# Down projections of a two-layer decoder trunk: the high weights' two products joined into one of 512 columns

## Chip, cores and metric

The kernel runs on one core of a Trainium2 chip. The metric is the time of one execution on the device in microseconds, the median of several runs. The kernel before takes 1029.28 us (three runs, 1028.52 to 1032.02).

## The reference

Two layers over 256 tokens of width 1024, all in float32. Each layer has a mixer (a gated delta-rule branch with 8 heads, a sliding-window attention branch with 16 heads, and an output projection) and a gated MLP of width 2816 with a causal convolution. Both are conditioned: a vector c gives six modulation vectors for each layer. The part that matters here is the end of each layer:

```python
h = rms_norm(x, norm_ffn[l]) * (1.0 + sc2) + sh2
up_act, up_lin = jnp.split(h @ w_up[l], 2, axis=-1)
up_act = causal_dwconv(up_act, ffn_conv[l]) + ffn_conv_b[l]
x = x + gt2 * ((jax.nn.silu(up_act) * up_lin) @ w_down[l])
```

The change touches the product with `w_down`, the multiplication by `gt2` and the addition to x.

## The kernel before

**Layout.** x lies in SBUF as 8 tiles of 128 features by 256 tokens. A projection gives one output tile (128 features by 256 tokens) at a time: the weights are the stationary side, 128 x 128 for each k tile, and the activations the moving side, 256 columns.

**Three products for one.** To keep the accuracy of float32 with the faster type fp32r, every operand is split into a high part (rounded to fp32r) and a low part (the rest). A projection adds up high x high, high weights x low activations, and low weights x high activations; `mm3` (lines 281 to 284) issues these three for each k tile, in this order, into one PSUM tile:

```python
PE.matmul(o, wh, ah, start=first, stop=False)
PE.matmul(o, wh, al, start=False, stop=False)
PE.matmul(o, wl, ah, start=False, stop=last)
```

**Weights.** They come in chunks of 128 x 1024 float32 (8 k tiles) through a pool `raw` of 6 buffers, loaded by SyncE's queue (line 200). ScalarE casts a chunk to its high part `wH` (line 210), and VectorE subtracts to get the low part `wL` (line 212); each of these pools has 4 buffers. `weights()` hands out the next chunk and starts what is three chunks ahead. Two offsets (`SHIFT`) inside the wH and wL tiles alternate by a table `KICK`; chunks 0 and 12 of each layer's down projection have the second.

**The MLP.** For 22 tiles of the inner width the kernel computes both up projections, convolution and gate, and stores the result in `gp[i]`, a tile of 128 x 2 x 256: the high part at index 0, the low part at index 1, so that the two lie side by side (lines 1162 to 1204). They stand in the profile as `g_a` (i below 8) and `g_b`.

**The down projection** (lines 1210 to 1229) runs over 8 output tiles f. For each f three chunks of 8, 8 and 6 k tiles go through `mm3` into a PSUM tile of 256 columns, alternately from the pool `acc` and from `dnps` (3 buffers each, one PSUM bank of 512 float32 columns per buffer). Then one VectorE instruction, the eviction in line 1221, computes x = p * gt2 + x:

```python
V.scalar_tensor_tensor(x[:, f], p_, mod[l][:, 40 + f:41 + f], x[:, f], op0=ALU.mult, op1=ALU.add)
```

What follows differs by layer. In layer 0, ScalarE squares the new x tile (line 416), VectorE adds the squares up for the next norm (line 417), ScalarE makes the fp32r part `xH` (line 430) and VectorE its low part `xL` (line 431), and layer 1 begins with products of `xH` and `xL` whose last k tile needs the tile f = 7. In layer 1, the x tile is stored to `out` (line 1229).

**Modulation of the next layer.** In layer 0's down projection, `ada_step` fetches rows of `w_ada` into the same `raw` pool and lets VectorE multiply and sum them (line 328): 15 times in f = 1 to 5 and once in f = 6.

**What sets the order.** A scheduler fixes each engine's order when the program is built, by priorities (`tc.high_priority`) and its own estimates; the engines then work through their queues in order. Evictions, squares and `xH`/`xL` have a high priority, loads and splits of weights that of work done ahead.

Of the kernel before, what the change touches and what calls it, by code (L numbers as in the profile page):

```python
# [8 lines left out]
ALU = mybir.AluOpType  # L9
# [4 lines left out]
T = 256  # L14
# [5 lines left out]
FT = FF // P  # L20
# [79 lines left out]
def trunk(tc, xT, cvec, pos, wada, wsa, wbig, wdn, par, cst, out):  # L100
    nc = tc.nc
    V, A, G, PE = nc.vector, nc.scalar, nc.gpsimd, nc.tensor
# [20 lines left out]
    def acc(w=T, name="acc"):  # L123
        return accp.tile([P, w], F32, name=name, tag="acc")

    def ps(shape, name="ps"):
        return dnp.tile([P] + list(shape), F32, name=name, tag="dn")
# [23 lines left out]
    x = cp.tile([P, KT, T], F32, name="x")  # L151
# [64 lines left out]
    def weights():  # L216
        i = nextc["i"]
        nextc["i"] += 1
        while state["n"] < min(len(plan), i + 1 + LOOK):
            with tc.high_priority(offset=AHEAD):  # L220
                load_chunk(state["n"])
                split_chunk(state["n"])
            state["n"] += 1
        return got.pop(i)
# [56 lines left out]
    def mm3(o, wh, wl, ah, al, first, last):  # L281
# [4 lines that stand above are left out]
    def proj(ah, al, w=T, alt=False):  # L286

        wh, wl = weights()
        wh = wh.rearrange("p (k n) -> p k n", n=P)
        wl = wl.rearrange("p (k n) -> p k n", n=P)  # L290
        p_ = ps([w], name="acc2") if alt else acc(w)
        for kt in range(KT):
            mm3(p_, wh[:, kt], wl[:, kt], ah(kt), al(kt), kt == 0, kt == KT - 1)
            tick(BLOCK)
        return p_


    mod = [cp.tile([P, 48], F32, name=f"mod{l}") for l in range(NL)]
# [43 lines left out]
    def need(l, g, lo, hi):  # L342
        assert all((l, g, i) in done for i in range(lo, hi)), (l, g, lo, hi)
# [19 lines left out]
    def ada_step(n=1):  # L363

        for _ in range(n):
            while adaq and len(adaf) < 2:
                l, g, f = adaq.pop(0)
                adaf.append((l, g, f, ada_fetch(l, g * 8 + f)))
            if adaf:
                l, g, f, raw = adaf.pop(0)  # L370
                dot = ada_dot(l, g * 8 + f, raw)
                if behind:
                    after(dot, behind["op"])
                if f % 4 == 3:
                    ada_cols(l, g, f - 3, f + 1)
# [33 lines left out]
    def ssq_add(kt):  # L409
        if kt == 0:  # L410
            s = wk.tile([P, T], F32, name="ssq", tag="ssq", bufs=1)
            A.activation(s, x[:, 0], AF.Square)
            ssq["t"] = s
        else:
            q = t1("sqx")
            A.activation(q, x[:, kt], AF.Square)
            V.tensor_tensor(ssq["t"], ssq["t"], q, ALU.add)
# [106 lines left out]
    for l in range(NL):  # L524
# [6 lines left out]
        if l:  # L531
            ga[0] = quad("ga0")
            for f in range(4):
                with tc.high_priority(offset=HPN):
                    nrm.tile(f)
                t, c = rawx.proj(nrm.r, 0.5)
# [34 lines left out]
        else:  # L571
            for i in range(12):
# [4 lines left out]
                wh, wl = (t.rearrange("p (k n) -> p k n", k=2) for t in weights())  # L577
                for k4 in range(2):
                    kt = i // 3 * 2 + k4
# [57 lines left out]
        for q4 in range(4):  # L637
# [6 lines left out]
            for j in range(4):  # L644
# [3 lines left out]
                                   op0=ALU.mult, op1=ALU.add)  # L648
            exps.append(A.activation(dmat[:, q4 * 4:q4 * 4 + 4], dmat[:, q4 * 4:q4 * 4 + 4], AF.Exp))

        def at(t):
            return lambda kt: t[:, kt]
# [473 lines left out]
        for f in range(8):  # L1126
            y_ = yb[f // 4][:, f % 4]
            p_ = proj(at(sH), at(sL))
# [33 lines left out]
        gp = []  # L1162
# [7 lines left out]
        gH = lambda i: gp[i][:, 0]  # L1170
        gL = lambda i: gp[i][:, 1]
# [7 lines left out]
        for i in range(FT):  # L1179
# [8 lines left out]
            with tc.high_priority(offset=hpe):  # L1188
                g = t1("g")
                A.activation(g, pa_, AF.Identity, scale=fw[:, i, 2:3], bias=PR(l, "fbias", i, i + 1))  # L1190
                for sft in (1, 2):
                    V.scalar_tensor_tensor(g[:, sft:], pa_[:, :T - sft], fw[:, i, 2 - sft:3 - sft], g[:, sft:],  # L1192
                                           op0=ALU.mult, op1=ALU.add)
                A.activation(g, g, AF.Silu)
            if i < 2:
                t, c = rawx.proj(nrm.r, alt=True)
                V.scalar_tensor_tensor(g, t, c, g, op0=ALU.add, op1=ALU.mult)
            else:
                p_ = proj(at(hh), at(hl), alt=True)
# [8 lines left out]
        if l + 1 < NL:  # L1208
            rawx = Raw(a1[l + 1], mod[l + 1][:, 0:8])
        for f in range(8):  # L1210
            p_ = ps([T], name="acc2") if f % 2 else acc()
            for a, b in DSPLIT:
                wh, wl = weights()
                wh = wh.rearrange("p (k n) -> p k n", n=P)
                wl = wl.rearrange("p (k n) -> p k n", n=P)
                for kt in range(a, b):
                    mm3(p_, wh[:, kt - a], wl[:, kt - a], gH(kt), gL(kt), kt == 0, kt == FT - 1)
                if l + 1 < NL and 0 < f < 7 and (f < 6 or a == 0):
                    ada_step()
            with tc.high_priority(offset=HPN):  # L1220
                V.scalar_tensor_tensor(x[:, f], p_, mod[l][:, 40 + f:41 + f], x[:, f], op0=ALU.mult, op1=ALU.add)
            if l + 1 < NL:
                with tc.high_priority(offset=HPN):
                    ssq_add(f)
                    need(l + 1, 0, f, f + 1)
                    need(l + 1, 1, f, f + 1)
                    rawx.tile(f)
            else:
                nc.sync.dma_start(out[:, f], x[:, f])
# [86 lines left out]
```

## Time and profile before

| | |
|---|---|
| median of three runs | 1029.28 us |
| profiled execution, its span | 1029.4 us |
| granted TensorE clock | 0.995 |
| layer 0, down projection | from 463.15 us, eight tiles |
| layer 1, down projection | from 965.72 us, eight tiles |
| mean DMA rate | 204 GB/s |

A profile's row of the timeline has the start in us from the span's start, the duration in us, the engine, the line, the operation with its tiles (out<-in), and what ended the idle time before it in brackets. PE is TensorE's products and PEld its weight loads, DVE is VectorE, ACT ScalarE, SPq SyncE's queue. A matmul row gives rows*columns of the array, then partitions x columns of the moving side. The ends of products are modelled, so durations of neighbours overlap; the distance of their starts is what a product costs in a row of products.

### The profile page before, as it was taken

To read this page: it belongs to the slowest core of one execution; us is meant where nothing else is said; L and a number is where in the kernel's file an instruction comes from. 1 tells how busy PE (TensorE), PEld (TensorE's weight loads), DVE (VectorE), ACT (ScalarE), POOL (GpSimd) and SP (SyncE) were. 2 spreads that over 40 slices of the span, in tenths; PEclk is the share of its full clock that TensorE was granted. 3 is DMA by queue.
4 is the path that set the end of the run, shared out by engine and by line. 5 is a ranking of instruction groups with operands and counts; after the bars stand their busy time and mean duration, and the time that the engine had idled before them with its cause. 6 is when DMAs were issued, how large, how long until landed. Compare 5 with 4: busy or idle time off the path is not lost.

```text
span 1029.4 us, 23195 instructions
## 1 busy us (share of the span) xinstructions
PE 999.7 (97%) x9208; PEld 946.0 (92%) x9208; DVE 843.6 (82%) x1873; ACT 631.2 (61%) x1281; POOL 4.0 (0%) x8
## 2 busy tenths in 40 slices
PE   4999999999999999999999999999999999999998
PEld 2599998998899999999999999899879999999998
DVE  6799997799788898998996999986857889777653
ACT  5598675766555665564465977577554558555532
POOL 0000000000000000000000000000000000000000
PEclk9999998999999999999999999999999999999999
DMA  9875486537555478888976556762313655566661
GB/s 361 324 247 175 173 268 204 183 124 266 170 183 191 155 226 282 291 282 298 358 262 210 168 168 193 239 242 83 110 57 107 202 185 179 191 191 194 185 211 40
DMA packets 60444, 210.47 MB, mean 204 GB/s; under 512 B 6960, under 2 KB 8496, under 8 KB 60336
## 3 DMA queue, kind: packets, MB, share of 16 engines
q1 hardware_dynamic: 59904, 208.89, 61.3%
q8 instruction: 72, 1.18, 0.5%
q14 instruction: 36, 0.29, 0.1%
q10 hardware_dynamic: 432, 0.10, 0.0%
HBM read 207.92 MB, written 1.05 MB: 203 GB/s over the span
## 4 chain that ended last, share of the span: by engine, by line
PE 77%; DVE 13%; ACT 5%; DMA 2%; issue 2%; SPq 0%; DVEq 0%; ACTq 0%
PE acc L282 20%; PE acc L283 19%; PE acc L284 19%; DVE wL L212 4%; PE pa L567 4%; DMA raw<-wada 2%; ACT wH L210 2%; DVE raw L328 2%; PE ps_o L1031 1%; PE ps_kk L728 1%; DVE kq L672 1%; PE ps_cur L975 1%; PE pa L585 1%; PE pa L583 1%; PE pa L584 1%
## 5 line engine op out<-in xcount | busy, mean ns | idle before, releaser
L210 ACT CAST wH<-raw 128x1024 fp32r<-128x1024 f32 (+2 forms) x292 | 301.0, 1035 | 207.8 <-PE acc L283 130.0
L212 DVE TENSOR_TENSOR wL<-raw,wH 128x1024 fp32r<-128x1024 f32 (+2 forms) x292 | 349.3, 1200 | 76.2 <-ACT wH L210 73.3
L282 PE MATMUL acc<-hH,wH 128*128 128x256 f32 x1376 | 394.3, 287 | 0.0
L283 PE MATMUL acc<-hL,wH 128*128 128x256 f32 x1376 | 385.8, 280 | 0.0
L284 PE MATMUL acc<-hH,wL 128*128 128x256 f32 x1376 | 385.1, 280 | 0.3 <-DVE wL L212 0.2
L282 PEld LDWEIGHTS acc<-hH,wH 128*128 128x128 f32 x1376 | 259.9, 189 | 7.4 <-issue 4.3
L284 PEld LDWEIGHTS acc<-hH,wL 128*128 128x128 f32 x1376 | 260.1, 189 | 1.1 <-DVE wL L212 0.7
L283 PEld LDWEIGHTS acc<-hL,wH 128*128 128x128 f32 x1376 | 260.1, 189 | 0.7 <-issue 0.2
L328 DVE SCALAR_TENSOR_TENSOR raw<-raw,cact 128x1024 f32<-128x1024 f32 x80 | 97.1, 1219 | 9.2 <-DMA raw<-wada 9.1
L284 PE MATMUL acc<-g_b,wL 128*128 128x256 f32 x224 | 61.8, 276 | 0.0
L282 PE MATMUL acc<-g_b,wH 128*128 128x256 f32 x224 | 61.8, 276 | 0.0
L283 PE MATMUL acc<-g_b,wH 128*128 128x256 f32 x224 | 61.8, 276 | 0.0
L672 DVE SCALAR_TENSOR_TENSOR kq<-cr,pt,kq 128x255 f32<-128x255 f32 (+2 forms) x96 | 45.4, 479 | 1.5 <-ACT kq L670 1.5
L282 PEld LDWEIGHTS acc<-g_b,wH 128*128 128x128 f32 x224 | 42.1, 188 | 0.0
L283 PEld LDWEIGHTS acc<-g_b,wH 128*128 128x128 f32 x224 | 42.1, 188 | 0.0
L284 PEld LDWEIGHTS acc<-g_b,wL 128*128 128x128 f32 x224 | 42.1, 188 | 0.0
L567 PE MATMUL pa<-raw,h 128*128 128x432 f32 x96 | 37.5, 555 | 2.6 <-ACT h L473 2.6
L1192 DVE SCALAR_TENSOR_TENSOR g<-acc,pt,g 128x255 f32<-128x255 f32 x80 | 38.2, 478 | 0.6
L567 PEld LDWEIGHTS pa<-raw,h 128*128 128x128 f32 x96 | 19.2, 202 | 20.6 <-issue 17.2
L282 PE MATMUL acc<-sH,wH 128*128 128x256 f32 x128 | 36.7, 289 | 0.0
L284 PE MATMUL acc<-sH,wL 128*128 128x256 f32 x128 | 36.6, 287 | 0.0
L283 PE MATMUL acc<-sL,wH 128*128 128x256 f32 x128 | 36.5, 285 | 0.0
(329 smaller groups left out, 1964.0 us busy)
## 6 DMA issues: line engine op xcount, KB each, us to landing
raw<-wbig SPq DMA_DIRECT2D x232, 512.0 KB, 4.0
raw<-wada SPq DMA_DIRECT2D x80, 512.0 KB, 4.5
raw<-wdn SPq DMA_DIRECT2D x32, 512.0 KB, 4.5
raw<-wsa SPq DMA_DIRECT2D x24, 432.0 KB, 4.8
early<-wada SPq DMA_DIRECT2D x16, 512.0 KB, 8.5
raw<-wdn SPq DMA_DIRECT2D x16, 384.0 KB, 4.1
x<-xT SPq DMA_DIRECT2D x4, 256.0 KB, 4.2
out<-x SPq DMA_DIRECT2D x8, 128.0 KB, 3.0
```

The lines of the kernel that those rows point to most:

```text
L210: A.copy(h, raw)
L212: V.tensor_tensor(lo, raw, h.bitcast(F32), ALU.subtract)
L282: PE.matmul(o, wh, ah, start=first, stop=False)
L283: PE.matmul(o, wh, al, start=False, stop=False)
L284: PE.matmul(o, wl, ah, start=False, stop=last)
L328: return V.scalar_tensor_tensor(raw, raw, 1.0, cact, op0=ALU.mult, op1=ALU.mult, accum_out=modp[l][:, f:f + 1])
L567: PE.matmul(pa[g][tb], h32[:, tb * P:tb * P + P], w, start=n == 0, stop=n == KT - 1)
L583: PE.matmul(o, hh[:, kt, sl], wh[:, k4], start=kt == 0, stop=False)
L584: PE.matmul(o, hh[:, kt, sl], wl[:, k4], start=False, stop=False)
L585: PE.matmul(o, hl[:, kt, sl], wh[:, k4], start=False, stop=kt == KT - 1)
L672: V.scalar_tensor_tensor(dst[:, sft:], cr[:, :T - sft], w_[:, 3 - sft:4 - sft], dst[:, sft:], op0=ALU.mult, op1=ALU.add)
L1192: V.scalar_tensor_tensor(g[:, sft:], pa_[:, :T - sft], fw[:, i, 2 - sft:3 - sft], g[:, sft:], op0=ALU.mult, op1=ALU.add)
```

## The change

For each k tile the two products with the high weights become one. Its moving side is the whole `gp[kt]`, 512 columns: high and low activations side by side, so its result fills a whole PSUM bank, high x high in the first half, high weights x low activations in the second. The product of low weights and high activations goes to the first half. At the end two evictions add the halves to x, one after the other.

```diff
         for f in range(8):
-            p_ = ps([T], name="acc2") if f % 2 else acc()
+            p_ = (ps([2 * T], name="acc2") if f % 2 else acc(2 * T)).rearrange("p (a t) -> p a t", a=2)
             for a, b in DSPLIT:
                 wh, wl = weights()
...
                 for kt in range(a, b):
-                    mm3(p_, wh[:, kt - a], wl[:, kt - a], gH(kt), gL(kt), kt == 0, kt == FT - 1)
+                    PE.matmul(p_, wh[:, kt - a], gp[kt], start=kt == 0, stop=False)
+                    PE.matmul(p_[:, 0], wl[:, kt - a], gH(kt), start=False, stop=kt == FT - 1)
                 if l + 1 < NL and 0 < f < 7 and (f < 6 or a == 0):
                     ada_step()
             with tc.high_priority(offset=HPN):
-                V.scalar_tensor_tensor(x[:, f], p_, mod[l][:, 40 + f:41 + f], x[:, f], op0=ALU.mult, op1=ALU.add)
+                for part in range(2):
+                    V.scalar_tensor_tensor(x[:, f], p_[:, part], mod[l][:, 40 + f:41 + f], x[:, f],
+                                           op0=ALU.mult, op1=ALU.add)
```

On TensorE, in the first tile of layer 0's down projection (numbers tell k tiles and chunks apart), the order before:

```order
L284 MATMUL acc_6264<-g_b_4611,wL_6195 128x256
L282 MATMUL acc_6264<-g_b_4612,wH_6194 128x256
L283 MATMUL acc_6264<-g_b_4612,wH_6194 128x256
L284 MATMUL acc_6264<-g_b_4612,wL_6195 128x256
L282 MATMUL acc_6264<-g_b_4612,wH_6194 128x256
```

and of the changed program:

```order
L1218 MATMUL acc_6264<-g_b_4609,wL_6195 128x256
L1217 MATMUL acc_6264<-g_b_4610,wH_6194 128x512
L1218 MATMUL acc_6264<-g_b_4610,wL_6195 128x256
L1217 MATMUL acc_6264<-g_b_4610,wH_6194 128x512
L1218 MATMUL acc_6264<-g_b_4611,wL_6195 128x256
```

Three products of 256 columns have become one of 512 and one of 256 (a `g_b` buffer holds two k tiles).

On VectorE, at the end of layer 0's down projection, from the eviction of f = 5 to that of f = 6 (`raw,modp<-raw,cact` is a dot product for the modulation), the order before:

```order
L1221 SCALAR_TENSOR_TENSOR x<-acc_6770,mod_102,x 128x256
L348 TENSOR_TENSOR mod_103<-modp_105,pt 128x4
L352 SCALAR_TENSOR_TENSOR a_1_110<-mod_103,pt 128x4
L212 TENSOR_TENSOR wL<-raw,wH 128x1024
L417 TENSOR_TENSOR ssq<-ssq,sqx 128x256
L431 SCALAR_TENSOR_TENSOR xL<-x,a_1_108,xH 128x256
L328 SCALAR_TENSOR_TENSOR raw,modp_105<-raw,cact 128x1024
L212 TENSOR_TENSOR wL<-raw,wH 128x1024
L212 TENSOR_TENSOR wL<-raw,wH 128x768
L1221 SCALAR_TENSOR_TENSOR x<-acc,mod_102,x 128x256
```

and now:

```order
L1223 SCALAR_TENSOR_TENSOR x<-acc_6665,mod_102,x 128x256
L212 TENSOR_TENSOR wL<-raw,wH 128x768
L1223 SCALAR_TENSOR_TENSOR x<-acc_6665,mod_102,x 128x256
L328 SCALAR_TENSOR_TENSOR raw,modp_105<-raw,cact 128x1024
L417 TENSOR_TENSOR ssq<-ssq,sqx 128x256
L431 SCALAR_TENSOR_TENSOR xL<-x,a_1_108,xH 128x256
L348 TENSOR_TENSOR mod_103<-modp_105,pt 128x4
L212 TENSOR_TENSOR wL<-raw,wH 128x1024
L352 SCALAR_TENSOR_TENSOR a_1_110<-mod_103,pt 128x4
L328 SCALAR_TENSOR_TENSOR raw,modp_105<-raw,cact 128x1024
L212 TENSOR_TENSOR wL<-raw,wH 128x1024
L1223 SCALAR_TENSOR_TENSOR x<-acc,mod_102,x 128x256
```

Each eviction stands twice, in places with a subtraction of weights between its halves, and a dot product has moved across an eviction.

On ScalarE, around the first two tiles of layer 0's down projection, the casts of weights and the two instructions on the new x stood like this:

```order
L210 CAST wH<-raw 128x1024
L412 ACTIVATE ssq<-x 128x256
L430 ACTIVATE xH<-x,a_1_108 128x256
L210 CAST wH<-raw 128x1024
L210 CAST wH<-raw 128x768
L210 CAST wH<-raw 128x1024
```

and now:

```order
L210 CAST wH<-raw 128x1024 x2
L412 ACTIVATE ssq<-x 128x256
L430 ACTIVATE xH<-x,a_1_108 128x256
L210 CAST wH<-raw 128x768
L210 CAST wH<-raw 128x1024
```

One cast has moved ahead of the instructions that wait for x. SyncE's order is the same, and on VectorE and ScalarE the order outside layer 0's down projection is too, but for the second evictions of layer 1.

## The prediction

> **What bounds the kernel now.** I read the page first: busy times, then the chain that ended last.
>
> ```profile
> PE 999.7 (97%) x9208; PEld 946.0 (92%) x9208; DVE 843.6 (82%) x1873; ACT 631.2 (61%) x1281; POOL 4.0 (0%) x8
> PE 77%; DVE 13%; ACT 5%; DMA 2%; issue 2%; SPq 0%; DVEq 0%; ACTq 0%
> ```
>
> TensorE's products make up most of the end, but VectorE stands in the chain too. The two stretches that the change touches, the down projections of layer 0 and of layer 1, have to be read apart. The view by stretches of time gives, for a late part of the first and for the whole of the second, busy us (and instructions) of PE, PEld, DVE, ACT and POOL, then the granted clock, the DMA share and GB/s:
>
> ```profile
> 482.63:524.48 41.85, 41.45 (x364) 41.25 (x363) 40.73 (x67) 21.32 (x30) 0.96 (x1) 1.00 0.97 356
> 965.70:1025.70 60.00, 60.00 (x530) 60.00 (x528) 28.40 (x31) 21.20 (x23) 0.00 (x0) 1.00 0.48 143
> ```
>
> Layer 1 is bound by TensorE alone: it never pauses, and VectorE is idle half of the time. In layer 0 TensorE, VectorE (40.73 of 41.85 us) and the DMA engines (0.97) are full together, since 16 dot products for the next layer's modulation run there. What VectorE does in that stretch, by groups (count, busy us, mean ns, idle before):
>
> ```profile
> L212 DVE TENSOR_TENSOR wL<-raw,wH 128x1024 fp32r<-128x1024 f32 (+1 forms) x19 | 21.3, 1136 | 0.0
> L328 DVE SCALAR_TENSOR_TENSOR raw<-raw,cact 128x1024 f32<-128x1024 f32 x12 | 14.7, 1221 | 1.0 <-DMA raw<-wada 1.0
> L1221 DVE SCALAR_TENSOR_TENSOR x<-acc,mod,x 128x256 f32<-128x256 f32 x6 | 2.9, 479 | 0.0
> ```
>
> Whether VectorE already holds up TensorE is told by single rows of the timeline (start, duration):
>
> ```profile
> 486.50 0.39 PE L284 MATMUL acc<-g_a,wL 128*128 128x256 f32 x1 [0.40 <-DVE wL L212]
> 517.89 2.09 DVE L212 TENSOR_TENSOR wL<-raw,wH 128x1024 fp32r<-128x1024 f32 x2
> 519.39 0.28 PE L284 MATMUL acc<-g_b,wL 128*128 128x256 f32 x1
> ```
>
> At 486.50 a product with low weights waited for its subtraction. At 517.89 the low weights of the chunk used from 519.39 were begun; a subtraction of this form takes 1.22 us (a row of it is shown further down), so they were done at 519.11, 0.28 us ahead of use. So there is next to no cover left in layer 0.
>
> **The change part by part.** The sum is made against the profiled execution's 1029.4 us; the median of the runs shown, 1029.28, is 0.1 us away, so nothing is added between them.
>
> *TensorE.* There are 2 x 8 x 22 = 352 steps (layer, output tile, k tile). Three 256 column products become one of 512 and one of 256; a weight load goes. Durations of single products overlap, so the price is the distance of starts. Below are first and last rows of unbroken rows of products: 18 steps of the 256 column product in the down projection, 13 steps of a 432 column one, 22 steps of a 256 column one in an up projection, 20 steps of a 258 column one.
>
> ```profile
> 979.78 0.28 PE L282 MATMUL acc<-g_b,wH 128*128 128x256 f32 x1
> 981.82 0.28 PE L282 MATMUL acc<-g_a,wH 128*128 128x256 f32 x1
> 557.80 0.36 PE L585 MATMUL pa<-wH,hL 128*128 128x432 f32 x1
> 560.34 0.36 PE L583 MATMUL pa<-wH,hH 128*128 128x432 f32 x1
> 861.54 0.28 PE L284 MATMUL acc<-hH,wL 128*128 128x256 f32 x1
> 864.13 0.28 PE L282 MATMUL acc<-hH,wH 128*128 128x256 f32 x1
> 531.20 0.28 PE L284 MATMUL acc<-xH,wL 128*128 128x258 f32 x1
> 533.62 0.29 PE L283 MATMUL acc<-xL,wH 128*128 128x258 f32 x1
> 717.99 1.02 PE L728 MATMUL ps_kk<-kq 128*128 128x256 f32 x4
> L728 PE MATMUL ps_kk<-kq 128*128 128x256 f32 x64 | 16.6, 378 | 0.0
> ```
>
> 256 columns: 2.04 / 18 = 113.3 ns, so 340.0 ns for today's step. 432 columns: 2.54 / 13 = 195.4 ns. Per column that is 0.443 and 0.452 ns: a wider product is not cheaper per column here. No row has 512 columns of this type, so I bound them. Low end: the plain fp32 product of 256 columns (the x4 row: 1.02 us less one duration of 378 ns, over 3) starts every 214 ns. That is about twice today's product, as if its 256 columns went through twice, and so the cheapest row for 512; with it a step is 214 + 113.3 = 327.3 ns. High end: the line through 113.3 and 195.4 (0.466 ns per column) gives 195.4 + 80 x 0.466 = 232.7 ns, and the 256 column product can also run at 2.59 / 22 = 117.7 ns, a second cadence which the same shape shows in the fifth and sixth row, together 350.4 ns. I take 512 x 0.443 = 226.7 ns, a step of 340.0: the 432 column row, the nearest in width, is on the side of no gain. So TensorE: 0 in layer 1, with ends 176 x -12.7 ns = -2.2 us and 176 x +10.4 ns = +1.8 us. In layer 0 a gain has nowhere to go (next term).
>
> The Trainium skill, page "TensorE: Matmul & The Clock Gate", section "Back-to-back issue gap", would price a product of N columns at N / 2.4 + 2.5 ns, an estimate of 215.8 for 512 and 109.2 for 256. The rows are above it, 113.3 at 256 and 195.4 at 432 (182.5 by the rule), so I don't use it for the sum; by it a step would be 325.0 against 327.5 ns and layer 1 would gain 0.4 us. The same section's figure for a sustained stream, about 131 ns at 512 columns, is below what 432 columns take here.
>
> *VectorE in layer 0.* Each output tile's eviction becomes two: 8 more instructions. What one costs in a full queue is the distance to the next start:
>
> ```profile
> 499.49 0.48 DVE L1221 SCALAR_TENSOR_TENSOR x<-acc,mod,x 128x256 f32<-128x256 f32 x1
> 499.88 1.22 DVE L212 TENSOR_TENSOR wL<-raw,wH 128x1024 fp32r<-128x1024 f32 x1
> DVE raw L328 <- DMA raw<-wada: 3.1, 5, 1.1
> 473.87 1.23 DVE L328 SCALAR_TENSOR_TENSOR raw<-raw,cact 128x1024 f32<-128x1024 f32 x1 [1.12 <-DMA raw<-wada]
> 475.02 0.48 DVE L1221 SCALAR_TENSOR_TENSOR x<-acc,mod,x 128x256 f32<-128x256 f32 x1
> ```
>
> 0.39 us, so 8 x 0.39 = 3.1 us more on an engine without room. The only slack is five pauses for modulation weights, 3.1 us in all, of which the longest (1.1) ends at 473.87, before the first eviction at 475.02; 2.0 us are left to absorb. That is no free room: a weight buffer is reloaded only once VectorE has freed it, so a later VectorE makes later loads, except where the DMA engines themselves are behind: at 0.97 busy and 356 GB/s (the stretch above) a load of 0.52 MB takes 1.5 us of them whatever was issued when. I take 1.5 of the 2.0 as absorbed and hence **+1.6 us**, ends +1.1 (all absorbed) and +3.1 (none). The scheduler's moves of one cast and one dot product add no instruction. The delay reaches TensorE where layer 1 begins: its first products need the last tile of x.
>
> ```profile
> 524.48 0.48 DVE L1221 SCALAR_TENSOR_TENSOR x<-acc,mod,x 128x256 f32<-128x256 f32 x1
> 525.33 0.50 ACT L430 ACTIVATE xH<-x,a 128x256 fp32r<-128x256 f32 x1
> 526.62 0.48 DVE L431 SCALAR_TENSOR_TENSOR xL<-x,a,xH 128x256 fp32r<-128x256 f32 x1
> 527.43 0.28 PE L283 MATMUL acc<-xL,wH 128*128 128x258 f32 x1
> ```
>
> Eviction, cast, low part, product: behind the last eviction everything is in line, and from 527.43 on TensorE has no pause in which the delay could be made good. TensorE's own speed in layer 0 is covered by this wait.
>
> *The tail.* In layer 1 the additional evictions lie under TensorE (28.40 of 60.00 us busy), but for the last:
>
> ```profile
> 1025.68 0.28 PE L284 MATMUL acc<-g_b,wL 128*128 128x256 f32 x1
> 1026.00 0.48 DVE L1221 SCALAR_TENSOR_TENSOR x<-acc,mod,x 128x256 f32<-128x256 f32 x1 [7.00 <-PE acc L284]
> 1026.51 0.33 SPq L1229 DMA_DIRECT2D out<-x  x1
> ```
>
> The second half reads the x that the first wrote, so it begins when that is done: **+0.5 us** before the output can leave.
>
> Sum: 1029.4 + 0 + 1.6 + 0.5 = **1031.5 us**.
>
> **The rivals.** *A wide product pays its fixed cost once.* Of the 113.3 ns, 256 columns at the plain product's pace (half of 214) would be 107; the rest, 6.3, would be paid per product. A weight load also lasts nearly as long as that: 134 ns for 64 columns and 188 for 128 mean 0.84 ns per column, 108 ns for 128, so the weight path is as full as the array, and a third of its work goes.
>
> ```profile
> L849 PEld LDWEIGHTS ps_z<-um,yt x64: 129/135/135, 181.8 to 763.6; 64*64 64x64 f32 x64
> L282 PEld LDWEIGHTS acc<-g_b,wH 128*128 128x128 f32 x224 | 42.1, 188 | 0.0
> ```
>
> Then a step takes 327 to 334 ns, layer 1 gains 1.1 to 2.2 us, and the result is 1029.3 to 1030.4. Against it stands the 432 column row: at that pace 432 columns are 181 ns, and the excess is 15 ns, not 6. The Trainium skill's gap rule is of this kind (a fixed cost per product), with the smaller gain named above.
>
> *The slow cadence* (ends slower). The same 256 column product runs at 113.3 or at 117.7 ns in long rows, and the 258 column ones take 2.42 / 20 = 121.0 ns. If alternating widths keep the stream out of the good cadence in layer 1, a step costs 345 to 350 ns: +0.9 to +1.8 us there, to 1032.4 to 1033.3. It is slower by over 0.3% from a step of 345 ns on. For it: no mixed row of widths exists in the trace, and all widths that are not 256 are worse per column. Against it: after the stall at 486.50 the good cadence comes back by itself, 16 steps in 1.81 us, 113.1 ns.
>
> ```profile
> 487.20 0.28 PE L283 MATMUL acc<-g_a,wH 128*128 128x256 f32 x1
> 489.01 0.28 PE L284 MATMUL acc<-g_a,wL 128*128 128x256 f32 x1
> ```
>
> *VectorE has room after all.* If the scheduler's new order or earlier loads absorb all 3.1 us, only the tail is left: 1029.9.
>
> *The change doesn't do what it says*: were the wide product split again, TensorE would be as before, which is the forecast's own value; the built program has it as one instruction of 512 columns.
>
> **How the numbers follow.** A measurement of this kernel tells about 0.3%, 3.1 us, from no change: 1026.2 to 1032.4. Forecast 47%, its own range 1031.0 to 1033.0 by VectorE's ends, a quarter of it above 1032.4. Fixed cost 22%, 1029.3 to 1030.4. Slow cadence 18%, nearly all slower. VectorE has room 9%, 1029.9. A gain of both (the low end of the step, and no cost on VectorE) 4%: 1029.4 - 2.2 + 0.5 = 1027.7, or a little less. Faster by over 0.3%: 3%; within: 69%; slower: 28%. The range from 1029.2 to 1033.8 leaves out part of the last case and the sum of both high ends (1029.4 + 1.8 + 3.1 + 0.5 = 1034.8).
>
> **What would show it.** Starts of the 512 and the 256 column products in layer 1: a step of 340 ns is right, under 335 is the fixed cost, over 345 the slow cadence. In layer 0: waits of PE for wL, VectorE at over 0.98 until about 525, and the low part of the last x tile beginning at 528.2 instead of 526.62. In the tail: two evictions, the second 0.5 us behind the first. The prediction is wrong if layer 0 shows no new waits of TensorE, or if layer 1's down projection lasts much less or more than 60.0 us.

## The result, and the profile after

The changed kernel takes 1038.79 us (median of 6 executions, 1033.63 to 1041.20), the kernel before beside it 1032.05 us (6 executions, 1028.52 to 1033.32): a ratio of 1.0074, 95% interval 1.0049 to 1.0099. A second comparison, described below, gave 1.0051 (1.0032 to 1.0070). The change makes the kernel slower by about 0.5 to 0.7%, 5 to 8 us. The prediction had 1031.5 us, 2 us more than before, in a range up to 1033.8.

The profiled execution took 1037.77 us, its span is 1035.6 us, its granted clock 0.994. Its page has these busy times and shares of the chain:

```profile
PE 1004.4 (97%) x8856; PEld 934.4 (90%) x8856; DVE 849.8 (82%) x1889; ACT 630.8 (61%) x1281; POOL 4.0 (0%) x8
PE 72%; DVE 16%; ACT 6%; issue 3%; DMA 3%; SPq 0%; DVEq 0%; ACTq 0%
```

There are 352 products fewer, and yet TensorE is busy for 4.7 us more (999.7 before). Where, the view by stretches shows. Each stretch goes from the start of the first product of a down projection to that of its last; first layer 0, then layer 1 (busy us and instructions of PE, PEld, DVE, ACT, POOL, then clock, DMA share, GB/s):

```profile
463.31:525.79 62.48, 62.27 (x353) 53.99 (x352) 59.07 (x105) 30.29 (x46) 0.95 (x1) 1.00 0.93 328
969.29:1031.29 62.00, 62.00 (x354) 53.98 (x352) 31.52 (x38) 21.14 (x23) 0.00 (x0) 1.00 0.48 138
```

In layer 1 TensorE never pauses, at full clock, and takes 62.00 us where the three narrow products took 59.96 (965.72 to 1025.68). By the mean distances of starts that is 352.9 ns for a step instead of 341.4 (three times 113.8). The weight path has become emptier, 53.98 us busy, and nothing is won by it. The starts in a row of steps of the changed kernel (timeline of PE):

```profile
999.66 0.40 PE L1217 MATMUL acc<-g_b,wH 128*128 128x512 f32 x1
999.90 0.28 PE L1218 MATMUL acc<-g_b,wL 128*128 128x256 f32 x1
1000.01 0.39 PE L1217 MATMUL acc<-g_b,wH 128*128 128x512 f32 x1
...
1003.17 0.39 PE L1217 MATMUL acc<-g_b,wH 128*128 128x512 f32 x1
```

Ten steps take 3.51 us, 351 ns each. Over the whole stretch a wide product is followed by the narrow one after 234.0 ns on average, the narrow one by the next wide one after 118.9. Both are dearer than forecast (226.7 and 113.3).

The tail (timeline of PE, DVE and SyncE's queue):

```profile
1031.29 0.28 PE L1218 MATMUL acc<-g_b,wL 128*128 128x256 f32 x1
1031.60 1.00 DVE L1223 SCALAR_TENSOR_TENSOR x<-acc,mod,x 128x256 f32<-128x256 f32 x2 [6.76 <-PE acc L1218]
1032.63 0.33 SPq L1232 DMA_DIRECT2D out<-x  x1
```

Two evictions in 1.00 us instead of one in 0.48, so the store leaves half a microsecond later. From the last product's start to the end of the span it is 4.34 us; before it was 3.75.

### The profile page after: what moved, and what is told of

The parts are those of the page before. It is cut to its first block, busy times and chain, and to the rows that moved or that the text cites. A ratio compares the mean times of both kernels' runs of the same rounds, so it can differ in the third digit from the quotient of the medians.

```text
span 1035.6 us, 22512 instructions
## 1 busy us (share of the span) xinstructions
PE 1004.4 (97%) x8856; PEld 934.4 (90%) x8856; DVE 849.8 (82%) x1889; ACT 630.8 (61%) x1281; POOL 4.0 (0%) x8
## 4 chain that ended last, share of the span: by engine, by line
PE 72%; DVE 16%; ACT 6%; issue 3%; DMA 3%; SPq 0%; DVEq 0%; ACTq 0%
PE acc L282 16%; PE acc L283 16%; PE acc L284 15%; DVE wL L212 6%; PE acc L1217 5%; PE pa L567 4%; DVE raw L328 2%; DMA raw<-wada 2%; PE acc L1218 2%; ACT wH L210 2%; DVE kq L672 1%; PE ps_cur L975 1%; PE ps_o L1031 1%; PE pa L585 1%; PE pa L583 1%
## 5 line engine op out<-in xcount | busy, mean ns | idle before, releaser
L1217 PE MATMUL acc<-g_b,wH 128*128 128x512 f32 x224 | 79.7, 396 | 0.0
L1217 PEld LDWEIGHTS acc<-g_b,wH 128*128 128x128 f32 x224 | 42.1, 188 | 10.2
L1217 PE MATMUL acc<-g_a,wH 128*128 128x512 f32 x128 | 46.0, 396 | 0.0
L1218 PE MATMUL acc<-g_a,wL 128*128 128x256 f32 x128 | 36.2, 283 | 0.2 <-DVE wL L212 0.2
```

The costliest lines, as they stand in the source:

```text
L1217: PE.matmul(p_, wh[:, kt - a], gp[kt], start=kt == 0, stop=False)
L1218: PE.matmul(p_[:, 0], wl[:, kt - a], gH(kt), start=False, stop=kt == FT - 1)
```

## The experiments

The changed kernel differs from before in two ways: in the width of the products, and in the second eviction of each tile. The first four runs separate the two, and the two layers.

**Narrow halves.** The two evictions stay, and the wide product is two of 256 columns again, one for each half of the bank:

```diff
-                    PE.matmul(p_, wh[:, kt - a], gp[kt], start=kt == 0, stop=False)
+                    PE.matmul(p_[:, 0], wh[:, kt - a], gH(kt), start=kt == 0, stop=False)
+                    PE.matmul(p_[:, 1], wh[:, kt - a], gL(kt), start=False, stop=False)
                     PE.matmul(p_[:, 0], wl[:, kt - a], gH(kt), start=False, stop=kt == FT - 1)
```

> The changed kernel with the 512 column product taken apart again: three products of 256 columns, the low activations' one into the second half of the bank, and both evictions kept. Theory A (the width alone spoils TensorE's cadence): a step is back at 340 ns, layer 1's down projection lasts 60.0 us from first to last product instead of 62.0, and only what the second evictions cost is left: 0.5 us in the tail and 1.1 to 3.1 us in layer 0, total 1.6 to 3.6 us over the kernel before. Rival B (the second half of the bank, being written in turn with the first, spoils the cadence whatever the width): a step stays at 350 ns or more and layer 1 at 62.0 us. Rival C (the evictions cost nothing in layer 0 because the wait at its end is set elsewhere): 0.5 us over the kernel before.

Measured: 1031.69 us, ratio 1.0005 (0.9981 to 1.0028). The two down projections in the view by stretches:

```profile
463.92:525.91 61.99, 61.53 (x530) 61.09 (x528) 58.54 (x104) 29.71 (x45) 0.97 (x1) 1.00 0.93 329
968.41:1028.38 59.97, 59.97 (x530) 59.97 (x528) 31.56 (x38) 21.21 (x23) 0.00 (x0) 1.00 0.47 143
```

Layer 1 is back at 59.97 us with two evictions per tile and with results in both halves of a bank. So in layer 1 the evictions, and the bank that is filled, cost TensorE nothing; the width does. Of layer 0 one profile says that two evictions per tile, with TensorE at its old pace, come out at 61.99 us, inside what the kernel before takes there (60.66 to 63.34 us in three profiles, shown below). The time as a whole is what rival C expected: about 0.5 us over the kernel before.

**One eviction.** The wide product stays, and the second half of the bank is not added to x (the product of high weights and low activations is left out of the sum):

```diff
-                for part in range(2):
+                for part in range(1):
```

> The changed kernel with the first eviction alone, so the products of low activations are left out of x. Theory A (width): layer 1's down projection stays at 62.0 us, the step at 353 ns; layer 0's delay is what TensorE's 13 ns a step add there, 176 x 13 = 2.3 us less the stall of 0.7 us that the kernel before has, 1.6 us; the tail is back at the time before: total about 2.0 + 1.6 = 3.6 us over the kernel before, plus what the middle of layer 1 may add. Rival (VectorE's second evictions make layer 0's delay): layer 0 ends as before, within 0.4 us, total 2.0 us.

Measured: 1038.27 us, ratio 1.0063 (1.0042 to 1.0083).

```profile
460.70:522.71 62.01, 62.01 (x354) 53.99 (x353) 58.10 (x101) 31.19 (x47) 0.96 (x1) 1.00 0.94 337
966.30:1028.30 62.00, 62.00 (x354) 53.97 (x352) 28.38 (x31) 21.14 (x23) 0.00 (x0) 1.00 0.46 138
```

With VectorE relieved of the second evictions both stretches stay at 62.0 us. In layer 0 TensorE is busy throughout: there too its products set the pace, and VectorE does not. The time is 6.5 us over the kernel before where 3.6 were expected; 2.0 us in layer 1 and the 62.0 us in layer 0 do not explain all of it, and the granted clock of these ten executions was lower (0.9943 against 0.9964).

The two runs together say more than the stages do. With the products narrow again the loss is gone (an interval up to 1.0028); with the second evictions gone it stays (an interval from 1.0042). So the loss as a whole goes with the wide product, not only the 2.0 us of layer 1.

**One layer at a time.** The changed form in layer 1 alone, then in layer 0 alone (`wide = l == 1`, `wide = l == 0`, with the code of before in the other layer; the PSUM tile and the evictions follow `wide` in the same way):

```diff
+            wide = l == 1
...
+                    if wide:
                         PE.matmul(p_, wh[:, kt - a], gp[kt], start=kt == 0, stop=False)
                         PE.matmul(p_[:, 0], wl[:, kt - a], gH(kt), start=False, stop=kt == FT - 1)
+                    else:
+                        mm3(p_, wh[:, kt - a], wl[:, kt - a], gH(kt), gL(kt), kt == 0, kt == FT - 1)
```

> The change in layer 1 alone. Theory A: all is as before up to layer 1's down projection, which lasts 62.0 us instead of 60.0, and the tail costs 0.5 us: 2.5 us over the kernel before. The 1.6 us that the middle of layer 1 (640 to 705 us) lost in the changed kernel are gone, if they come from where layer 0 ended. Rival (the middle's loss comes from the built order or from chance): it is there again, total 4.1 us.

> The change in layer 0 alone. Theory A: layer 1 begins 1.9 us late as in the changed kernel, the middle of layer 1 loses its 1.6 us again, and layer 1's down projection lasts 60.0 us: 3.5 us over the kernel before. Rival (the middle's loss is chance): 1.9 us.

Measured: layer 1 alone 1033.64 us, ratio 1.0027 (1.0002 to 1.0052); layer 0 alone 1033.01 us, ratio 1.0016 (0.9997 to 1.0036). Layer 1's down projection in the two:

```profile
964.10:1026.09 61.99, 61.99 (x353) 53.98 (x352) 31.52 (x38) 21.14 (x23) 0.00 (x0) 1.00 0.45 138
968.50:1028.46 59.96, 59.96 (x529) 59.96 (x528) 28.37 (x31) 21.20 (x23) 0.00 (x0) 1.00 0.48 144
```

Layer 1's 2.0 us come and go with the wide product in that layer. By the ratios each layer has a part of the loss, 2.8 and 1.7 us over the kernel before, together 4.5, a little less than the 5 to 8 us of both at once; for layer 0 alone the interval still includes no loss at all.

**Width or alternation?** A step is dear either because a wide product is, or because widths alternate. Three runs tell these apart. The first sorts the products of each chunk, all wide ones ahead of all narrow ones:

```diff
                 for kt in range(a, b):
                     PE.matmul(p_, wh[:, kt - a], gp[kt], start=kt == 0, stop=False)
+                for kt in range(a, b):
                     PE.matmul(p_[:, 0], wl[:, kt - a], gH(kt), start=False, stop=kt == FT - 1)
```

> In each chunk all 512 column products come first, then all 256 column ones (6 or 8 of each in a row); everything is computed. Theory 'alternation' (it is the change of width from product to product that costs): the distance of starts in a row of 512 column products is 226.7 ns, in a row of 256 column ones 113.3, and layer 1's down projection lasts 60.0 to 60.4 us from its first to its last product. Theory 'width' (a 512 column product costs more than two of 256 whatever its neighbours): 512 columns 231 to 236 ns, 256 columns back at 113.3, a step of 345 to 349 ns, 60.7 to 61.5 us. If both stay where the alternating row has them (234.5 and 118.5 ns), 62.0 us, and neither theory explains the narrow product. Time against the kernel before: ratio 1.001 by alternation, 1.003 to 1.005 by width.

Measured: 1035.42 us, ratio 1.0043 (1.0016 to 1.0071); layer 1's down projection 60.94 us (969.45 to 1030.38), 347 ns for a step. Its rows (timeline of PE, here with equal neighbours gathered in one row, their number at the end):

```profile
999.97 2.02 PE L1217 MATMUL acc<-g_a,wH 128*128 128x512 f32 x8
1001.84 1.11 PE L1219 MATMUL acc<-g_a,wL 128*128 128x256 f32 x8
1002.78 2.00 PE L1217 MATMUL acc<-g_b,wH 128*128 128x512 f32 x8
1004.62 1.07 PE L1219 MATMUL acc<-g_b,wL 128*128 128x256 f32 x8
1005.52 0.85 PE L1217 MATMUL acc<-g_b,wH 128*128 128x512 f32 x3
```

Eight wide products take 1.87 and 1.84 us, 234 and 230 ns each; eight narrow ones 0.94 and 0.90 us, 117.5 and 112.5 ns. Over the whole stretch wide is followed by wide after 230.9 ns, narrow by narrow after 115.9. About half of the loss in layer 1 is gone, 1.0 of 2.0 us. Of the half that stays, about 0.6 us lie in the wide products and 0.4 us in the narrow ones, which are still above their 113.8. Both theories hold a part.

The second leaves out the products with the low weights, so that wide ones alone remain (one execution, 1023.79 us, with less work than the others):

```diff
-                    PE.matmul(p_, wh[:, kt - a], gp[kt], start=kt == 0, stop=False)
-                    PE.matmul(p_[:, 0], wl[:, kt - a], gH(kt), start=False, stop=kt == FT - 1)
+                    PE.matmul(p_, wh[:, kt - a], gp[kt], start=kt == 0, stop=kt == FT - 1)
```

> Leaves out the products of low weights with high activations in both down projections, so that unbroken rows of 512 column products alone remain (the low weights are still worked out and not used). Theory 'alternation': starts 226.7 ns apart. Theory 'width': 231 to 236 ns apart. Time is not compared: a third of the products is gone, 176 x 113 to 118 ns = 20 to 21 us per layer at most, in layer 0 less because VectorE and the loads then set the pace.

```profile
999.69 2.94 PE L1217 MATMUL acc<-g_b,wH 128*128 128x512 f32 x12
1002.46 2.03 PE L1217 MATMUL acc<-g_a,wH 128*128 128x512 f32 x8
1004.33 2.02 PE L1217 MATMUL acc<-g_b,wH 128*128 128x512 f32 x8
```

Twelve in 2.77 us, then eight in 1.87: 231 and 234 ns, on average 231.8 over the stretch. So the price of a 512 column product in a row of its kind is 231.8 ns, 0.453 per column, the price per column that the 432 column product had before (0.452).

The third has two products of 384 columns for each k tile, as many columns and products as in the changed kernel, but one width. It leaves out high weights with the second half of the low rows, adds low weights with low rows, and its second eviction adds columns 128 to 383 to x, so it tells of time alone (one execution, 1032.72 us). Against the kernel before:

```diff
-                    mm3(p_, wh[:, kt - a], wl[:, kt - a], gH(kt), gL(kt), kt == 0, kt == FT - 1)
+                    m = gp[kt].rearrange("p a t -> p (a t)")[:, 0:384]
+                    PE.matmul(p_[:, 0:384], wh[:, kt - a], m, start=kt == 0, stop=False)
+                    PE.matmul(p_[:, 0:384], wl[:, kt - a], m, start=False, stop=kt == FT - 1)
...
+                for part in range(2):
+                    V.scalar_tensor_tensor(x[:, f], p_[:, 128 * part:128 * part + T], mod[l][:, 40 + f:41 + f], x[:, f],
+                                           op0=ALU.mult, op1=ALU.add)
```

> Per k tile two products of 384 columns (high weights, then low weights, each on the high rows and the first half of the low rows): as many columns, products and weight loads as in the changed kernel, but no change of width. Leaves out the product of the high weights with the second half of the low rows, and adds one of low weights with low rows in its place. Theory 'alternation': starts 384 x 0.443 = 170.0 ns apart, a step of 340.0 ns, layer 1's down projection 60.0 us as before. Theory 'width': on the line between 113.3 ns at 256 and 234.5 at 512 columns, 173.9 ns, a step of 348 ns, 61.2 us; if the amount on top is one per product wider than 256 (7.8 ns each), 177.8 ns and 62.6 us.

```profile
999.75 0.34 PE L1219 MATMUL acc<-g_b,wL 128*128 128x384 f32 x1
1003.24 0.33 PE L1219 MATMUL acc<-g_b,wL 128*128 128x384 f32 x1
965.07:1026.20 61.13, 61.13 (x353) 61.13 (x352) 31.21 (x38) 21.17 (x23) 0.00 (x0) 1.00 0.47 140
```

Twenty distances in 3.49 us are 174.5 ns, and the stretch lasts 61.13 us, as the theory of width had it (173.9 ns, 61.2 us). That is 0.453 ns per column again. So 256 columns at 113.3 ns are the exception, 0.443 per column; 384, 432 and 512 columns cost 0.452 to 0.453.

**Is one profile enough for layer 0?** The stretch from layer 1's first product of line 583 to its down projection was 1.6 us longer in the first profile of the changed kernel (430.55 us instead of 428.95), though the change does not touch it. And the run with the change in layer 1 alone, whose layer 0 is the code of before, had 61.79 us there, where the first profile of before had 60.66. So both kernels were profiled again (the changed one in an execution of 1037.73 us, the one before in executions of 1032.06 and 1034.91 us).

> The changed kernel once more, for a second profile. If the 1.6 us more between layer 0's and layer 1's down projection (430.55 us against 428.95 before) belong to the change, they come back; if they belong to the single execution, this stretch lies anywhere from 428 to 430.6. The down projections themselves (62.0 to 62.5 us and 62.0 us) come back in either case.

> The kernel before once more, for a second profile. Theory 'change': what lies between the two down projections costs the same as in the first profile, 428.95 us (1.7 less if no spell of half clock falls into it, 1.7 more if one is twice as long), and the 1.6 to 2.1 us more of the changed kernel's two profiles belong to its layer 0. Theory 'execution': the waits of TensorE for vv and yt of ScalarE near 654 and 677 us differ from one execution to the next, and this stretch comes out up to 2 us longer without any change. Layer 0's down projection: 60.7 us as in the first profile, or up to 61.8, as in the kernel with the wide product in layer 1 alone, whose layer 0 is the same program.

> The kernel before a third time, with the same expectations as for its second profile: two executions tell whether a difference of 1 us in the stretch between the down projections, or in layer 0's down projection, is more than one execution's chance. Layer 1's down projection 59.96 us in each.

Layer 0's down projection, three times before and then twice after (the fifth row is from the last comparison below):

```profile
463.15:523.81 60.66, 60.26 (x529) 60.06 (x528) 56.47 (x98) 29.92 (x46) 0.96 (x1) 1.00 0.93 336
462.84:526.18 63.34, 61.54 (x530) 60.75 (x528) 57.47 (x98) 30.75 (x47) 0.95 (x1) 1.00 0.93 325
465.96:529.28 63.32, 60.90 (x529) 60.50 (x528) 57.90 (x99) 31.09 (x47) 0.95 (x1) 1.00 0.93 326
463.18:525.28 62.10, 62.10 (x353) 53.97 (x352) 59.69 (x105) 30.96 (x47) 0.96 (x1) 1.00 0.94 332
464.57:526.57 62.00, 62.00 (x353) 53.99 (x352) 58.63 (x103) 29.93 (x45) 0.95 (x1) 1.00 0.95 336
```

The one profile that the prediction had was a lucky execution: 60.66 us, where two others of the same program took 63.3. In those TensorE waited longer for low weights (0.4 us in the first profile); the view of waits has for the second and the third profile of before (us in all, times, longest):

```profile
PE acc L284 <- DVE wL L212: 1.8, 3, 0.9
PE acc L284 <- DVE wL L212: 2.4, 2, 1.2
```

In the changed kernel TensorE is busy all the time and needs 62.0 to 62.5 us, less than before's bad executions and more than its good one. The delay of the changed kernel comes later. Up to 655 us the longest wait of VectorE for a load in layer 1 is one for modulation weights, near 635 us. Its rows, three of before and three of after:

```profile
632.24 1.23 DVE L328 SCALAR_TENSOR_TENSOR raw<-raw,cact 128x1024 f32<-128x1024 f32 x1 [0.67 <-DMA raw<-wada]
634.21 1.23 DVE L328 SCALAR_TENSOR_TENSOR raw<-raw,cact 128x1024 f32<-128x1024 f32 x1 [0.50 <-DMA raw<-wada]
637.50 1.23 DVE L328 SCALAR_TENSOR_TENSOR raw<-raw,cact 128x1024 f32<-128x1024 f32 x1 [0.51 <-DMA raw<-wada]
634.62 1.23 DVE L328 SCALAR_TENSOR_TENSOR raw<-raw,cact 128x1024 f32<-128x1024 f32 x1 [1.07 <-DMA raw<-wada]
635.12 1.22 DVE L328 SCALAR_TENSOR_TENSOR raw<-raw,cact 128x1024 f32<-128x1024 f32 x1 [2.24 <-DMA raw<-wada]
636.50 1.22 DVE L328 SCALAR_TENSOR_TENSOR raw<-raw,cact 128x1024 f32<-128x1024 f32 x1 [2.43 <-DMA raw<-wada]
```

Counted from the first product of layer 0's down projection (the left bounds above, 463.31 for the first profile after), this instruction starts at 169.1, 171.4 and 171.5 us before, at 171.3, 171.9 and 171.9 after. What the changed kernel does not lose to waits in layer 0 it loses here: the data for this instruction are there no earlier, and the pause grows from 0.5 or 0.7 to 1.1 to 2.4 us. VectorE's later results then hold up TensorE, which some 19 us later waits for `vv`, a tile of layer 1's mixer that ScalarE makes, and ScalarE waits for VectorE. The view of waits from 640 to 662 us (us in all, times, longest), three of before and three of after:

```profile
PE ps_vt L703 <- ACT vv L674: 2.3, 1, 2.3
PE ps_vt L703 <- ACT vv L674: 1.8, 1, 1.8
PE ps_vt L703 <- ACT vv L674: 2.1, 1, 2.1
PE ps_vt L703 <- ACT vv L674: 2.7, 1, 2.7
PE ps_vt L703 <- ACT vv L674: 3.9, 1, 3.9
PE ps_vt L703 <- ACT vv L674: 4.0, 1, 4.0
```

On average that is 3.5 us instead of 2.1. But not every execution of the wide form loses this: the run with the change in layer 0 alone, whose VectorE and ScalarE orders are the changed kernel's up to layer 1's down projection, came to the modulation load 170.1 us after its start, paused 0.6 us, and TensorE's wait was 2.3 us. Whether it is the loads as such that fix this time was not tried by a run of its own.

Right behind that wait comes a second difference. All three profiles of the changed kernel have a spell of half clock near 655 us, of before's only the first (at 652). The same stretch in the last profile after and the second before:

```profile
656.20:659.60 3.40, 3.40 (x19) 3.40 (x18) 2.79 (x6) 2.01 (x4) 0.00 (x0) 0.51 0.76 258
656.20:659.60 3.40, 3.40 (x32) 3.40 (x31) 3.40 (x7) 1.72 (x4) 0.00 (x0) 1.00 0.92 264
```

19 products instead of 32, though not quite the same ones. Product by product, 256 columns start every 213 ns in the spell and every 113 outside it, so a spell of 3.4 us costs nearly half of itself, 1.7 us. The spells do not need a wide product: the run with narrow halves has one too, at 655.5 us behind a wait of 2.2 us, the run with layer 0 alone at 654.9 behind 2.3, while the 384 column run had a wait of 2.8 us and no spell. Between the first products of the two down projections it is 502.6, 503.7 and 503.5 us before and 506.0, 506.1 and 506.2 after, on average 2.8 us more. 1.1 of that are the spells (three of three against one of three, at 1.7), and 1.7 the rest. With layer 0 alone, one execution with a spell, it is 504.8. Both theories of these runs are half right: the longer stretch comes back in every profile of the changed kernel, and single executions of one program differ by more than 1 us.

**Does the wide product draw more spells?** So the changed kernel was timed once more, in five rounds, for the granted clock of many executions, and with it the kernel with two products of 384 columns.

> The changed kernel timed once more beside the kernel before on one chip, for the granted clock of many executions. So far the mean granted clock over the executions is 0.9940 (7 of the changed kernel) against 0.9966 (44 of the kernel before, partly on other chips), and 0.001 of it goes with 0.9 to 1.0 us. Theory 'spells': the changed kernel draws more half clock spells; its mean stays at 0.993 to 0.995 while that of before, on this chip, is 0.996 to 0.9975, and the ratio is 1.006 to 1.008. Theory 'chance': the means agree within 0.0008, and the ratio is 1.004 to 1.0045, which is what the stages give at equal clock (2.0 in layer 1, 0.6 in the tail, 1.2 to 1.7 from layer 0 on).

> Two products of 384 columns for each k tile, timed (again without the product of the high weights with the second half of the low rows, and with one of low weights and low rows instead). Layer 1's down projection 61.1 us, 1.2 more than before, and the tail 0.6 more. Theory 'spells from wide products': the granted clock is lower here too, 0.994 to 0.995, and the ratio 1.004 to 1.006. If only rows with changing widths draw spells, or if it was chance: a clock within 0.0008 of before's and a ratio of 1.001 to 1.003.

Measured: the changed kernel 1037.41 us (9 executions), before 1030.70 (20), ratio 1.0051 (1.0032 to 1.0070); mean granted clock 0.9952 and 0.9960. With 384 columns 1035.80 us (12 executions, 1032.48 to 1043.25), ratio 1.0047 (1.0022 to 1.0071), mean clock 0.9953. The clocks lie 0.0008 and 0.0007 below before's, at the edge of what 'chance' had; the changed kernel's ratio falls between the two forecasts, and that of the 384 column kernel is what 'spells' had. The difference of 0.0026 seen earlier has mostly gone. On other chips the runs with one eviction and with sorted products were 0.0021 and 0.0020 below the kernel before beside them, and the one with narrow halves was 0.0009 above it. So it is not shown that wide products lower the clock, nor is it ruled out.

## Why the prediction was wrong

Forecast were four terms: 0 from TensorE, 1.6 us from VectorE in layer 0, 0.5 us in the tail, and no difference between the profiled execution and the median. Measured, by stages and on average over three profiles of each kernel:

| | predicted | measured |
|---|---|---|
| layer 1's down projection (TensorE) | 0 (-2.2 to +1.8) | +2.0 |
| layer 0's down projection and what follows, up to layer 1's | +1.6 (1.1 to 3.1) | +2.8, of it 1.1 by spells of half clock |
| tail | +0.5 | +0.6 |
| outside the span | 0 | +0.3 (1.8 us before, 2.1 after; cause open) |
| sum | +2.1 | +5.7, a ratio of 1.006 |

The stage ahead of layer 0's down projection, which the change does not touch, was 0.3 us shorter on average and is not in this sum.

**TensorE's step is the one that failed.** The prediction took "512 x 0.443 = 226.7 ns, a step of 340.0". The step took 352.9 ns, beyond even the high end of 350.4. The mis-sized term has two parts. First, the price per column was taken from the 256 column product, though the only row of much wider products that the prediction showed, 432 columns, had 0.452 ns; by it 512 columns are 231.4 ns, and rows of them alone took 231.8. The prediction saw this ("a wider product is not cheaper per column here") and read it as no gain where it meant a loss. Against the average narrow product of the layer (59.96 us over 527 distances, 113.8 ns) that makes 231.8 - 2 x 113.8 = 4.2 ns for a step, 0.7 us for 176. Second, alternation: 234.0 + 118.9 instead of 231.8 + 113.8 is 7.3 ns for a step, 1.3 us. Together 2.0 us. The argument that the good cadence "comes back by itself" after a stall was of no use, since it came from a row of one width.

The rival of the slow cadence was right in kind and direction (a step of 345 to 350 ns, over the bound from 345 on); it had 18%, and against it stood only that row after a stall. The rival of a fixed cost paid once fell: half of the loads of high weights are gone, the array's stream is longer all the same.

**Layer 0: a delay was right, its mechanism wrong.** The prediction let VectorE's eight evictions hold up layer 1 and said that "TensorE's own speed in layer 0 is covered by this wait". It is the other way round: with one eviction per tile the stretch lasted the same 62.0 us, TensorE was busy throughout, and in the changed kernel's three profiles no wait for low weights above 0.2 us is left in it. That the slower TensorE gives VectorE cover fits this, but the second evictions did not lengthen the stretch beyond before's with narrow products either (61.99 us, one profile). The forecast sign for a wrong mechanism, "if layer 0 shows no new waits of TensorE", came true. Of the delay up to layer 1's down projection, 1.7 us without the spells, the modulation load's instruction is later by 1.0 (171.7 us instead of 170.7, on average), and TensorE's wait for `vv` behind it longer by 1.5. That the one causes the other is read from their order in time. Why the load comes late in three profiles and not in the run with layer 0 alone stays open; that the wide product is behind the delay rests on the timed runs, where narrow halves lose nothing.

**The tail** was right: 0.59 us for 0.5.

**The base was too low.** The prediction set the profiled execution's 1029.4 us beside the median of 1029.28 and added nothing. But 1029.4 is a span. Where both are known, an execution takes 1.8 us more than its span (1032.06 and 1030.3 us in before's second profile), so the profiled execution belongs, by an estimate, to about 1031.2 us. The medians of before in the comparisons were 1030.7 to 1032.1 us. That is 1.8 us of the miss, and no part of the change.

**The range** was too narrow for two more reasons: executions of the same program lie between 1026.2 and 1036.2 us, while all bounds came from one profile; and the high end of TensorE's step was built of two rows of one width each, so it did not bound what alternating widths can add (234.0 + 118.9 against 232.7 + 117.7 ns).

## What to carry to other kernels

Joining two fp32r products of 256 columns into one of 512 saved a weight load that was hidden and made the stream longer: 231.8 ns against 2 x 113.8 in rows of one width, and another 7 ns for a step where widths alternate. Before joining products, price the wider one by the nearest wider row of the profile, per column, and treat a row of mixed widths as unknown on the dear side. And where several engines are full together, take a second profile of the kernel before: one execution can be the lucky one, and the stage that looks tight may wait by itself.

## What was unexpected of the hardware

- The 256 column fp32r product has the best price per column of the widths seen: 113.3 ns in a good row (0.443 ns per column), against 174.1 at 384 (0.453), 195.4 at 432 (0.452) and 231.8 at 512 (0.453).
- A change of width from product to product makes both dearer: 234.0 and 118.9 ns alternating, 230.9 and 115.9 in blocks of six or eight, 231.8 and 113.8 in rows of one width.
- The clock falls to one half for 3.4 us or multiples of it (6.8, 10.2, 17.1), in places that recur (near 167 and 655 us) but not in every execution. The spells near 655 us stand at TensorE's wait for `vv`, of 1.7 to 4.0 us in all fourteen profiles; four of them, with waits of 1.8 to 2.8 us, have no spell there. The kernel without the products of low weights in its down projections had the lowest clock of all profiles (0.986, one execution). In 31 executions of before on one chip the median span was 1032.2 us at a clock of 0.993 and 1028.7 us at 0.998.
